# Copying gated products by DMA into 32-bit rounded tiles and transposing them in that type

## The chip, the cores and the metric

The kernel runs on one core of a Trainium2 chip. The core's engines each follow their own instruction stream: TensorE (PE, with PEld for its loads of the stationary operand), VectorE (DVE), ScalarE (ACT), GpSimd (POOL) and SyncE (SP). Data moves between HBM, the on-chip memory SBUF and the accumulation banks PSUM; DMA transfers are issued by one of the engines and carried by 16 DMA engines. The metric is device time in microseconds (us), the median of several runs of the whole program.

## The reference

Two layers of an encoder block on 256 tokens of width 1024. Each layer is a feed-forward half step, two attention branches with gates, and a second feed-forward half step:

```python
for l in range(DEPTH):                                  # DEPTH = 2
    x = x + 0.5 * swiglu(rms_norm(x, ffn1_norm[l]), ffn1_w_gate[l], ffn1_w_up[l], ffn1_w_down[l])
    ...                                                 # neighbourhood and sliding-window attention, gates, w_out
    x = x + 0.5 * swiglu(rms_norm(x, ffn2_norm[l]), ffn2_w_gate[l], ffn2_w_up[l], ffn2_w_down[l])

def swiglu(x, w_gate, w_up, w_down):                    # widths 1024 -> 2816 -> 1024
    return (jax.nn.silu(x @ w_gate) * (x @ w_up)) @ w_down
```

The change touches the four `swiglu` calls: it concerns the product `silu(...) * (...)`, called the gated product here, on its way from the first two matmuls to the third.

## The kernel before, in words

**Numbers in two parts.** Every operand of a matmul is split into a high part rounded to the 32-bit type fp32r and a low part, the rest, also fp32r. `split_to` does it: ACT writes `hi` by a copy (L184), DVE writes `lo = src - hi` (L185). A product then takes three matmuls, hi·hi, hi·lo and lo·hi (`three`, L170 to L172); one such triple of 512 columns is one unit of the kernel's own clock, a tick.

**Feed-forward.** The 2816 middle columns are cut into 11 chunks of 256. For chunk c, `columns` brings the weights in four pieces of 512 KB, gate and up side by side, and `project` forms a 128x512 bank for each of the two token tiles t = 0 and 1: 8 triples a tile, 16 ticks a chunk. `glu` then makes the gated product: ACT applies Silu to one half of the bank (`sg`, L443), DVE multiplies it with the other (`hh`, L444). `hh` has two buffers, each with both token tiles of one chunk.

**The turn.** The third matmul needs the gated product with the middle columns on the partitions. `turn` lets PE transpose two chunks at once (the last chunk, c = 10, alone), as four 128x128 blocks a chunk, against an identity matrix `ident` in float32 (L320), into a PSUM bank `tp`. `arrange` then splits the bank into `hi` and `lo`; for eight of the chunks it first copies it into `a` (L330) and forms four sums for a seven-product scheme of block multiplication. The third matmul follows in `down`, which starts with chunk 0 (eight triples into `acc`).

**What sets the order.** PE's order is the order in which the code records its matmuls. A step that must wait for other engines is put off with `defer(lag, ...)`: it is recorded at the first tick that lies at least `lag` ticks after its call.

```python
H_LAG, NORM_LAG, QK_LAG, P_LAG, V_LAG, M_LAG = 7.9, 4.0, 16, 10, 7.5, 5.5
LAST_LAG = 6.1
...
waiting.append((c, pair[0]))
if c % 2 or c == NFC - 1:
    defer(LAST_LAG if c == NFC - 1 else H_LAG, ("h", c), lambda group=waiting: turn(group))
```

So a pair's turn stands 8 ticks, the last one 7 ticks, behind the last triple of its chunk. On the other engines a scheduler places the instructions. All weight loads are issued by SP into a ring of four raw buffers; a load waits until its buffer has been split, and the splits write a ring of six `wh`/`wl` tiles that PE gives free.

**The opening.** While the first rows of x are on their way, PE runs matmuls on a tile of zeros (`warmup`, L118 to L120): five, then the transposes of the first rows, five more, then the transposes of the rows of token tile 1, then three.

The names that the prediction uses: `hh` the gated product, `tp` the transposes' bank, `wh`, `wl` the parts of a weight piece, `corner`, `u`, `v` pieces of the down weights and their differences for the seven products, `raw` a buffer that a load fills. "FFN 0" to "FFN 3" are the four feed-forward steps in order of time.

Of the kernel before, what the change touches and what calls it, by code (L numbers as in the profile page):

```python
# [11 lines left out]
F32 = mybir.dt.float32  # L12
F32R = mybir.dt.float32r
I32 = mybir.dt.int32
BF16 = mybir.dt.bfloat16
# [6 lines left out]
P = 128  # L22
D = 1024
S = 256
# [5 lines left out]
NFC = FF // FC  # L30
# [10 lines left out]
RING = 6  # L41
RAW = 4
LAG = 3
H_LAG, NORM_LAG, QK_LAG, P_LAG, V_LAG, M_LAG = 7.9, 4.0, 16, 10, 7.5, 5.5
LAST_LAG = 6.1
MORE = {"Q1": 2, ("sw", 4): 1.5, ("na", 4): 2, ("na", 5): 1.5}
ORDER = ("Q0 Q1 K0 K1 q1 q0 a5 k0 a5 k1 a3 v0 a1 a5 v1 a3 g0 a1 a5 g1 a4 g2 a0 g3 a0 a4 g4 a1 a5 g5 a4 "
         "g6 a0 g7")
# [3 lines left out]
PLAN = "SFGFGGFGGSS"  # L52
PREP = {3: 1, 5: 3, 7: 6}
PREP_FIRST = {5: 1, 7: 3, 8: 6}
NS = sum(kind != "S" for kind in PLAN)
# [3 lines left out]
def hybrid_encoder(ctx, tc, x, w_gu1, w_d1, w_in, b_gate, qk_gain, rpb, sink, t5,  # L59
                   w_bna, w_bsw, w_out, w_gu2, w_d2, c_mask, c_band, out):  # L60
    nc = tc.nc
# [7 lines left out]
    ps_tp = ctx.enter_context(tc.tile_pool(name="ps_tp", bufs=2, space=PSUM))  # L69
# [9 lines left out]
    def fetch(t, h):  # L79
        if (t, h) == (0, 0):  # L80
            nc.sync.dma_start(wide[:, :HEAD + 512], x[:P, :HEAD + 512])
        else:
            nc.sync.dma_start(xs[t][:, h * 512:(h + 1) * 512],
                              x[t * P:(t + 1) * P, HEAD + h * 512:HEAD + (h + 1) * 512])
# [3 lines left out]
    ident = const.tile([P, P], F32, name="ident")  # L88
    make_identity(nc, ident)
    ident_r = const.tile([P, P], F32R, name="ident_r")  # L90
# [23 lines left out]
    blank = ring.tile([P, 2, 512], F32R, name="blank", tag="wl", bufs=RING)  # L114
    nc.vector.memset(blank[:, 0, :].bitcast(F32), 0.0)
    idle = ps_acc.tile([P, 512], F32, name="idle", tag="po")

    def warmup(n):  # L118
        for _ in range(n):
            nc.tensor.matmul(idle, blank[:, 0, :P], blank[:, 0, :], start=True, stop=True)  # L120

    chain = {}

# [15 lines left out]
    def load(src, nk, n):  # L139
        raw = ring.tile([P, 2, 512], F32, name="raw", tag="raw", bufs=RAW)  # L140
        r = raw[:, :nk, :n]
        nc.sync.dma_start(r, src)
        return parts(r, nk, n)

    def columns(w, l, c0, n, nk=KD):
        return [load(w[l, 2 * i * P:(2 * i + 2) * P, c0:c0 + n].rearrange("(k p) n -> p k n", p=P), 2, n)
                for i in range(nk // 2)]
# [7 lines left out]
    def defer(lag, key, fn):  # L155
        later.append((now[0] + lag, len(later), key, fn))
        later.sort(key=lambda e: e[0])
# [6 lines left out]
    def tick(cost):  # L164
        now[0] += cost
        while later and later[0][0] <= now[0]:
            later.pop(0)[3]()
# [15 lines left out]
    def split_to(hi, lo, src):  # L183
        linked("act", lambda: nc.scalar.activation(hi, src, AF.Copy))  # L184
        linked("dve", lambda: nc.vector.tensor_tensor(lo, src, hi.bitcast(F32), ALU.subtract))  # L185
# [7 lines left out]
    def norm(t, n, half, apart=False):  # L193
        if half == 0:
            xT[t] = [act.tile([P, KD, P], F32R, name=f"x{p}{t}", tag=f"x{p}{t}") for p in "hl"]
            ssq[t] = small.tile([P, 2], F32, name="ssq", tag="ssq")
        ks = slice(4 * half, 4 * half + 4)
        tp = ps_tp.tile([P, 4, P], F32, name="tp", tag="tp")
        for i in range(4):
            k = 4 * half + i  # L200
            nc.tensor.transpose(tp[:, i, :], xs[t][:, k * P:(k + 1) * P], ident)  # L201
        xg = act.tile([P, 4, P], F32, name="xg", tag="xg", bufs=2)
        if apart and half == 1:
            for i in range(4):
                linked("act", lambda: nc.scalar.activation(xg[:, i, :], tp[:, i, :], AF.Copy,
                                                           scale=gain[:, n, 4 + i:5 + i]))
        else:
            linked("dve", lambda: nc.vector.tensor_tensor(
                xg, tp, gain[:, n, ks].unsqueeze(2).to_broadcast([P, 4, P]), ALU.mult))
        split_to(*(x[:, ks, :] for x in xT[t]), xg)  # L210
        if not apart:
            square(t, half)
# [12 lines left out]
    def opening(w, l, early):  # L225
        def piece(i, c=0):
            return load(w[l, 2 * i * P:(2 * i + 2) * P, c * 512:(c + 1) * 512].rearrange("(k p) n -> p k n", p=P),
                        2, 512)

        ps = [ps_g.tile([P, 512], F32, name="g", tag="g") for _ in range(T)]  # L230

        def steps(t, i):
            wh, wl = pieces[i]
            xh, xl = xT[t]
            for a, b in ((xh, wh), (xl, wh), (xh, wl)):
                for k in (2 * i, 2 * i + 1):
                    nc.tensor.matmul(ps[t], a[:, k, :], b[:, k % 2, :], start=a is xh and b is wh and k == 0,
                                     stop=b is wl and k == KD - 1)
            tick(2)

        pieces = []
        chain["act"] = warmed
        warmup(5)
        norm(0, 0, 0, True)
        pieces.append(piece(0))
        warmup(5)
        fetch(1, 0)
        norm(1, 0, 0, True)
        pieces.append(piece(1))
        fetch(0, 1)  # L250
        fetch(1, 1)
        warmup(3)
        steps(0, 0)
        norm(0, 0, 1, True)
        steps(1, 0)
        pieces.append(piece(2))
        norm(1, 0, 1, True)
        pieces.append(piece(3))
        square(0, 0, idle)
        square(0, 1, idle)  # L260
        for i in (1, 2, 3):
            for t in range(T):
                steps(t, i)
        second = [piece(0, 1)]
        square(1, 0, idle)
        early(ps[0])
        second.append(piece(1, 1))
        square(1, 1, idle)
        second += [piece(i, 1) for i in range(2, KD // 2)]
        chain.clear()  # L270
        defer(24, "constants", constants)
        defer(70, "scaled", scaled)
        return ps, second
# [36 lines left out]
    def ffn(l, n, w_gu, w_d, after):  # L310
        with tc.tile_pool(name="ffn", bufs=1) as fp:
            hs = {}
            SLOT = ((1, 2), (0, 3))

            def turn(group):
                tps = [ps_tp.tile([P, 4, P], F32, name="tp", tag="tp") for _ in group]
                for (_, hh), tp in zip(group, tps):
                    for t in range(T):
                        for i in range(2):
                            nc.tensor.transpose(tp[:, SLOT[t][i], :], hh[:, t, i * P:(i + 1) * P], ident)  # L320
                for (c, _), tp in zip(group, tps):
                    arrange(c, tp)

            def arrange(c, tp):
                m = 4 if PLAN[c] == "S" else 7
                hi = fp.tile([P, m, P], F32R, name=f"hi{m}", tag=f"hi{m}", bufs=NS if m == 7 else NFC - NS)
                lo = fp.tile([P, m, P], F32R, name=f"lo{m}", tag=f"lo{m}", bufs=NS if m == 7 else NFC - NS)
                if m == 7:
                    a = fp.tile([P, 8, P], F32, name="a", tag="sums", bufs=2)
                    nc.scalar.activation(a[:, :4, :], tp, AF.Copy)  # L330
                    for to, x, y, op in ((4, 0, 3, ALU.add), (6, 1, 0, ALU.subtract), (5, 4, 1, ALU.subtract),
                                         (7, 2, 5, ALU.subtract)):
                        nc.vector.tensor_tensor(a[:, to, :], a[:, x, :], a[:, y, :], op)
                    split_to(hi, lo, a[:, 1:, :])
                else:
                    with tc.high_priority(150 if c == NFC - 1 else 0):
                        split_to(hi, lo, tp)
                hs[c] = (hi, lo)
# [108 lines left out]
            waiting = []  # L447
            for c in range(NFC):
                first = n == 0 and c == 0
                pair = [None]  # L450
                if first:
                    both, second = opening(w_gu, l, lambda ps: glu(0, ps, pair))
                elif n == 0 and c == 1:
                    pieces = second
                else:
                    pieces = columns(w_gu, l, c * 512, 512)
                prep = PREP if n else PREP_FIRST
                if c in prep:
                    prepare(prep[c])
                for t in range(T):  # L460
                    if not first:
                        glu(t, project(t, pieces, 512), pair)
                    elif t:
                        glu(t, both[t], pair)
                waiting.append((c, pair[0]))
                if c % 2 or c == NFC - 1:
                    defer(LAST_LAG if c == NFC - 1 else H_LAG, ("h", c), lambda group=waiting: turn(group))
                    waiting = []
# [376 lines left out]
```

## Time and profile before

| what | value |
|---|---|
| median of 3 runs | 1077.5 us (1076.47 to 1078.26) |
| profiled execution: span from first to last instruction | 1075.2 us; no time beside the span is given for this one execution |
| granted TensorE clock, mean | 0.999 |
| PE busy | 1068.2 us, 99% of the span, 5125 matmuls |
| PEld / DVE / ACT / POOL busy | 83% / 81% / 62% / 11% |
| DMA | 212.63 MB moved, mean 198 GB/s; all weight loads on one queue, which took 62.3% of the 16 engines' span |
| chain that ended last | PE 97%, DMA 1%, ACT 1% |

The profile shows one execution. A row of the timeline has start, duration, engine, source line, operation, `out<-in` and the count; what stands in brackets is the engine's idle time just before it and what ended that. Matmuls are pipelined: each lasts longer than the distance to the next, so the distance between starts is what one costs, and a busy PE is not PE at its peak.

### The profile page before, as it was taken

How to read it: one execution, taken by the hardware profiler on the slowest of the kernel's cores; microseconds unless marked ns; L12 is line 12 of the kernel's file. 1: busy time of each engine (PE TensorE's matmuls, PEld its weight loads, DVE VectorE, ACT ScalarE, POOL GpSimd, SP SyncE). 2: the span in 40 equal slices, each digit the busy share in tenths (PEclk: the TensorE clock that was granted, in tenths of full speed). 3: DMA queues.
4: the chain of work that ended last, by engine and by line, in shares of the span. 5: the costliest groups of instructions: out<-in, count | busy, mean ns of one | idle time of the engine just before them, and what ended most of it. 6: DMA issues, size and time to landing. Idle time of an engine off the chain costs nothing.

```text
span 1075.2 us, 14749 instructions
## 1 busy us (share of the span) xinstructions
PE 1068.2 (99%) x5125; PEld 890.3 (83%) x5125; DVE 875.8 (81%) x1337; ACT 671.5 (62%) x1014; POOL 116.7 (11%) x118
## 2 busy tenths in 40 slices
PE   8999999999999999999999999999999999999998
PEld 6888888888888888888888888888888888888887
DVE  6678799889886768869977887988898867778696
ACT  6566654788764556565565665557877646566552
POOL 1000120243520000000000000003534000000000
PEclk9999999999999999999999999999999999999999
DMA  7767656765654667756657765657666554776652
GB/s 247 227 214 237 215 190 191 228 194 155 192 188 137 198 199 246 242 168 191 214 162 238 227 213 185 199 153 247 177 195 185 176 175 160 237 231 203 188 196 89
DMA packets 98827, 212.63 MB, mean 198 GB/s; under 512 B 7568, under 2 KB 13744, under 8 KB 98752
## 3 DMA queue, kind: packets, MB, share of 16 engines
q1 hardware_dynamic: 98560, 211.60, 62.3%
q8 instruction: 40, 0.66, 0.2%
q14 instruction: 35, 0.29, 0.1%
q0 software_dynamic: 192, 0.08, 0.1%
HBM read 210.59 MB, written 1.06 MB: 197 GB/s over the span
## 4 chain that ended last, share of the span: by engine, by line
PE 97%; DMA 1%; ACT 1%; DVE 0%; issue 0%; SPq 0%; ACTq 0%
PE g L170 22%; PE g L172 22%; PE g L171 22%; PE acc L170 5%; PE acc L172 5%; PE acc L171 5%; PE tp L320 2%; PE sc L568 1%; PE po L603 1%; PE tp L170 1%; PE tp L171 1%; PE tp L172 1%; PE pt L589 1%; PE tp L201 1%; PE br L170 1%; PE br L171 1%
## 5 line engine op out<-in xcount | busy, mean ns | idle before, releaser
L185 DVE TENSOR_TENSOR wl<-raw,wh 128x1024 fp32r<-128x1024 f32 x336 | 405.7, 1219 | 65.5 <-ACT wh L184 61.8
L184 ACT ACTIVATE wh<-raw 128x1024 fp32r<-128x1024 f32 x336 | 346.7, 1045 | 117.3 <-DMA raw<-in_w_gu 51.4
L170 PE MATMUL g<-wh,xh 128*128 128x512 f32 (+1 forms) x976 | 383.1, 393 | 0.5 <-DVE hh L444 0.5
L172 PE MATMUL g<-wh,xl 128*128 128x512 f32 (+1 forms) x976 | 377.8, 387 | 0.0
L171 PE MATMUL g<-wl,xh 128*128 128x512 f32 (+1 forms) x976 | 377.5, 387 | 0.0
L172 PEld LDWEIGHTS g<-wh,xl 128*128 128x128 f32 x976 | 183.4, 188 | 39.1 <-DVE xl L185 1.5
L170 PEld LDWEIGHTS g<-wh,xh 128*128 128x128 f32 x976 | 183.6, 188 | 33.8 <-DVE hh L444 1.1
L171 PEld LDWEIGHTS g<-wl,xh 128*128 128x128 f32 x976 | 183.7, 188 | 33.4 <-DVE wl L185 0.6
L443 ACT ACTIVATE sg<-g,rs_y 128x256 f32<-128x256 f32 x88 | 41.1, 467 | 89.7 <-PE g L172 77.3
L444 DVE SCALAR_TENSOR_TENSOR hh<-g,rs_y,sg 128x256 f32<-128x256 f32 x88 | 42.3, 481 | 53.0 <-ACT sg L443 53.0
L170 PE MATMUL acc<-wh,hi 128*128 128x512 f32 x180 | 71.2, 395 | 0.0
L171 PE MATMUL acc<-wl,hi 128*128 128x512 f32 x180 | 70.2, 390 | 0.0
L172 PE MATMUL acc<-wh,lo 128*128 128x512 f32 x180 | 70.1, 390 | 0.0
L176 POOL TENSOR_TENSOR rs_y<-ms,mhalf 128x1 f32<-128x1 f32 x12 | 8.1, 678 | 556.5 <-DVE ms L222 548.0
L352 DVE TENSOR_TENSOR u<-raw 128x512 f32<-128x512 f32 x64 | 41.7, 686 | 20.9 <-DMA raw<-in_w_d 20.8
L184 ACT ACTIVATE corner<-raw 128x512 fp32r<-128x512 f32 x32 | 20.1, 629 | 40.4 <-DMA raw<-in_w_d 22.4
L581 POOL TENSOR_TENSOR S<-S,sm 128x512 f32<-128x512 f32 x32 | 37.2, 1161 | 65.6 <-DVE sm L580 38.3
L172 PEld LDWEIGHTS acc<-wh,lo 128*128 128x128 f32 x180 | 33.8, 188 | 7.2
L171 PEld LDWEIGHTS acc<-wl,hi 128*128 128x128 f32 x180 | 33.8, 188 | 6.7
L170 PEld LDWEIGHTS acc<-wh,hi 128*128 128x128 f32 x180 | 33.8, 188 | 6.7
L184 ACT ACTIVATE wh<-v 128x1024 fp32r<-128x1024 f32 x20 | 21.2, 1062 | 28.9 <-DVE v L352 24.5
L574 ACT ACTIVATE S<-S,mx 128x256 f32<-128x256 f32 x64 | 31.9, 499 | 8.0 <-DVE mx L571 7.9
(189 smaller groups left out, 1522.0 us busy)
## 6 DMA issues: line engine op xcount, KB each, us to landing
raw<-in_w_gu SPq DMA_DIRECT2D x176, 512.0 KB, 4.5
raw<-in_w_d SPq DMA_DIRECT2D x100, 512.0 KB, 4.2
raw<-in_w_in SPq DMA_DIRECT2D x64, 512.0 KB, 4.7
raw<-in_w_out SPq DMA_DIRECT2D x16, 512.0 KB, 3.6
bb<-in_b_gate SPq DMA_DIRECT2D x16, 256.0 KB, 3.6
raw<-in_w_bsw SPq DMA_DIRECT2D x8, 512.0 KB, 3.9
raw<-in_w_bna SPq DMA_DIRECT2D x8, 512.0 KB, 3.5
raw<-in_w_d SPq DMA_DIRECT2D x12, 256.0 KB, 2.7
```

Source lines behind the costliest of these rows:

```text
L170: nc.tensor.matmul(ps, xh, wh, start=first, stop=False)
L171: nc.tensor.matmul(ps, xh, wl, start=False, stop=False)
L172: nc.tensor.matmul(ps, xl, wh, start=False, stop=last)
L184: linked("act", lambda: nc.scalar.activation(hi, src, AF.Copy))
L185: linked("dve", lambda: nc.vector.tensor_tensor(lo, src, hi.bitcast(F32), ALU.subtract))
L201: nc.tensor.transpose(tp[:, i, :], xs[t][:, k * P:(k + 1) * P], ident)
L320: nc.tensor.transpose(tp[:, SLOT[t][i], :], hh[:, t, i * P:(i + 1) * P], ident)
L352: sub = lambda to, x, y: nc.vector.tensor_tensor(to, x, y, ALU.subtract)
L443: linked("act", lambda: nc.scalar.activation(sg, ps[:, :FC], AF.Silu, scale=rstd[t]))
L444: linked("dve", lambda: nc.vector.scalar_tensor_tensor(pair[0][:, t], ps[:, FC:], rstd[t], sg, op0=ALU.mult, op1=ALU.mult))
L574: nc.scalar.activation(S_[:, t, :], S_[:, t, :], AF.Exp, bias=mx[:, t:t + 1], scale=-1.0, accum_out=sm[:, t:t + 1])
L581: nc.gpsimd.tensor_tensor(S_, S_, sm.unsqueeze(2).to_broadcast([P, T, S]), ALU.mult)
```

## The change

1. As soon as the gated product of a chunk is complete, a DMA that ACT issues copies its bits, 128 partitions of 2 KB, into the first four blocks of that chunk's `hi` tile, whose type is fp32r (`bits`). There are 44 such copies, one for each of 11 chunks in four FFNs.
2. PE transposes from there, with the identity in fp32r (`ident_r`) and a bank of type fp32r. The bank is read as float32 afterwards; `hi` is then overwritten with the rounded high part as before.
3. `H_LAG` goes from 7.9 to 10 and `LAST_LAG` from 6.1 to 7.6, so that a pair's turn stands 10 ticks and the last one 8 ticks behind its chunk.
4. The second five warm-up matmuls become two in fp32r, four in bf16 and one in float32, all of 512 columns on the same zeros.

```diff
-H_LAG, NORM_LAG, QK_LAG, P_LAG, V_LAG, M_LAG = 7.9, 4.0, 16, 10, 7.5, 5.5
-LAST_LAG = 6.1
+H_LAG, NORM_LAG, QK_LAG, P_LAG, V_LAG, M_LAG = 10, 4.0, 16, 10, 7.5, 5.5
+LAST_LAG = 7.6
...
-    def warmup(n):
+    def warmup(n, kind=F32R):
+        zero = blank[:, 0, :].bitcast(kind)
         for _ in range(n):
-            nc.tensor.matmul(idle, blank[:, 0, :P], blank[:, 0, :], start=True, stop=True)
+            nc.tensor.matmul(idle, zero[:, :P], zero[:, :512], start=True, stop=True)
...
-        warmup(5)
+        warmup(2)
+        warmup(4, BF16)
+        warmup(1, F32)
         fetch(1, 0)
...
             def turn(group):
-                tps = [ps_tp.tile([P, 4, P], F32, name="tp", tag="tp") for _ in group]
-                for (_, hh), tp in zip(group, tps):
+                tps = [ps_tp.tile([P, 4, P], F32R, name="tp", tag="tp") for _ in group]
+                for (c, raw), tp in zip(group, tps):
                     for t in range(T):
                         for i in range(2):
-                            nc.tensor.transpose(tp[:, SLOT[t][i], :], hh[:, t, i * P:(i + 1) * P], ident)
-                for (c, _), tp in zip(group, tps):
-                    arrange(c, tp)
+                            nc.tensor.transpose(tp[:, SLOT[t][i], :], raw[:, 2 * t + i, :], ident_r)
+                for (c, raw), tp in zip(group, tps):
+                    arrange(c, raw, tp.bitcast(F32))
+
+            def halves(c, p):
+                m = 4 if PLAN[c] == "S" else 7
+                return fp.tile([P, m, P], F32R, name=f"{p}{m}", tag=f"{p}{m}", bufs=NS if m == 7 else NFC - NS)
+
+            def bits(c, hh):
+                hi = halves(c, "hi")
+                nc.scalar.dma_start(hi[:, :4, :].bitcast(F32), hh.rearrange("p t (i n) -> p (t i) n", i=2))
+                return hi
...
-                waiting.append((c, pair[0]))
+                waiting.append((c, bits(c, pair[0])))
```

On PE, the turn of chunks 0 and 1 in FFN 0; before, it stands behind the last triple of chunk 2's tile 0 (`g_371`):

```order
L170 MATMUL g_371<-wh_367,xh0_114 128x512
L171 MATMUL g_371<-wl_368,xh0_114 128x512
L172 MATMUL g_371<-wh_367,xl0_115 128x512
L320 MATMUL tp_396<-ident_83,hh_259 128x128 x4
L320 MATMUL tp_397<-ident_83,hh_315 128x128 x4
L170 MATMUL g_427<-wh_349,xh1_138 128x512
```

and now:

```order
L171 MATMUL g_409<-wh_355,xh1_140 128x512
L172 MATMUL g_409<-wl_356,xh1_140 128x512
L173 MATMUL g_409<-wh_355,xl1_141 128x512
L323 MATMUL tp_416<-ident_r_88,hi4_292 128x128 x4
L323 MATMUL tp_417<-ident_r_88,hi7_351 128x128 x4
L171 MATMUL g_409<-wh_361,xh1_140 128x512
```

It has moved two triples into tile 1 (`g_409`), and it reads `hi` tiles where it read `hh`.

On DVE, the instructions around the last gated product of FFN 0 (chunk 10, tile 1); before:

```order
L352 TENSOR_TENSOR u_1393<-raw_1384,raw_1382 128x512
L185 TENSOR_TENSOR corner_1350<-raw_1346,corner_1350 128x512
L352 TENSOR_TENSOR u_1393<-raw_1382 128x512
L444 SCALAR_TENSOR_TENSOR hh_1242<-g_1193,rs_y_214,sg_1243 128x256
L185 TENSOR_TENSOR corner_1386<-raw_1382,corner_1386 128x512
L333 TENSOR_TENSOR a_1230<-a_1230 128x128 x2
L185 TENSOR_TENSOR lo4_1239<-tp_1219,hi4_1238 128x512
L185 TENSOR_TENSOR wl_1354<-raw_1348,wh_1353 128x1024
L333 TENSOR_TENSOR a_1230<-a_1230 128x128
L185 TENSOR_TENSOR wl_1390<-raw_1384,wh_1389 128x1024
L333 TENSOR_TENSOR a_1230<-a_1230 128x128
L185 TENSOR_TENSOR wl_1397<-u_1393,wh_1396 128x1024
```

(`corner_1432` and then `hh_1242` of tile 1 follow), and now:

```order
L186 TENSOR_TENSOR corner_1363<-raw_1359,corner_1363 128x512
L454 SCALAR_TENSOR_TENSOR hh_1232<-g_1207,rs_y_216,sg_1233 128x256
L186 TENSOR_TENSOR corner_1399<-raw_1395,corner_1399 128x512
L362 TENSOR_TENSOR u_1406<-raw_1397,raw_1395 128x512
L362 TENSOR_TENSOR u_1406<-raw_1395 128x512
L186 TENSOR_TENSOR wl_1367<-raw_1361,wh_1366 128x1024
L343 TENSOR_TENSOR a_1254<-a_1254 128x128 x2
L186 TENSOR_TENSOR lo4_1262<-tp_1244,hi4_1181 128x512
L186 TENSOR_TENSOR wl_1403<-raw_1397,wh_1402 128x1024
L343 TENSOR_TENSOR a_1254<-a_1254 128x128
L186 TENSOR_TENSOR wl_1410<-u_1406,wh_1409 128x1024
L186 TENSOR_TENSOR corner_1445<-raw_1441,corner_1445 128x512
```

(`hh_1232` of tile 1 follows). Two `corner` pieces and tile 0's gated product have moved ahead of `u`, and one of the `a` sums has moved behind the last gated product.

On ACT, the same place; now:

```order
L185 ACTIVATE wh_1409<-u_1406 128x1024
L185 ACTIVATE corner_1445<-raw_1441 128x512
L453 ACTIVATE sg_1283<-g_1236,rs_y_275 128x256
L185 ACTIVATE corner_1477<-raw_1473 128x512
L333 DMA hi4_1286<-hh_1232 128x512
L185 ACTIVATE hi7_1098<-a_1254 128x896
L185 ACTIVATE hi4_1286<-tp_1351 128x512
```

The copy's issue stands behind one more piece of weights (`corner_1477`), and what stood behind that piece now stands behind the copy's issue.

More of the change, by code (lines that the diff above doesn't have):

```diff
@@ L315, in turn, with arrange @@
             def turn(group):
-                tps = [ps_tp.tile([P, 4, P], F32, name="tp", tag="tp") for _ in group]
-                for (_, hh), tp in zip(group, tps):
+                tps = [ps_tp.tile([P, 4, P], F32R, name="tp", tag="tp") for _ in group]
+                for (c, raw), tp in zip(group, tps):
                     for t in range(T):
                         for i in range(2):
-                            nc.tensor.transpose(tp[:, SLOT[t][i], :], hh[:, t, i * P:(i + 1) * P], ident)
-                for (c, _), tp in zip(group, tps):
-                    arrange(c, tp)
-            def arrange(c, tp):
+                            nc.tensor.transpose(tp[:, SLOT[t][i], :], raw[:, 2 * t + i, :], ident_r)
+                for (c, raw), tp in zip(group, tps):
+                    arrange(c, raw, tp.bitcast(F32))
+            def halves(c, p):
                 m = 4 if PLAN[c] == "S" else 7
-                hi = fp.tile([P, m, P], F32R, name=f"hi{m}", tag=f"hi{m}", bufs=NS if m == 7 else NFC - NS)
-                lo = fp.tile([P, m, P], F32R, name=f"lo{m}", tag=f"lo{m}", bufs=NS if m == 7 else NFC - NS)
-                if m == 7:
+                return fp.tile([P, m, P], F32R, name=f"{p}{m}", tag=f"{p}{m}", bufs=NS if m == 7 else NFC - NS)
[3 more added lines that the diff above has]
+                return hi
+            def arrange(c, hi, tp):
+                lo = halves(c, "lo")
+                if PLAN[c] != "S":
                     a = fp.tile([P, 8, P], F32, name="a", tag="sums", bufs=2)
```

## The prediction

> **What bounds the kernel now.** I read the page's busy times and its chain of waits first.
>
> ```profile
> PE 1068.2 (99%) x5125; PEld 890.3 (83%) x5125; DVE 875.8 (81%) x1337; ACT 671.5 (62%) x1014; POOL 116.7 (11%) x118
> PE 97%; DMA 1%; ACT 1%; DVE 0%; issue 0%; SPq 0%; ACTq 0%
> ```
>
> The chain is PE from the opening to the last store. So what PE's own stream loses is gained in full, a wait put into that stream is lost in full, and work on DVE, ACT or the queues counts only where PE comes to wait for it. The last place before PE waits is the splitting of weights, in the groups by line:
>
> ```profile
> L184 ACT ACTIVATE wh<-raw 128x1024 fp32r<-128x1024 f32 x328 | 342.1, 1055 | 116.7 <-DMA raw<-in_w_gu 51.4 <-PE g L172 37.4 <-PE acc L172 11.6
> ```
>
> ACT waits 51 us for loads and about as long for PE to free a tile; none of it reaches PE, because six split pieces lie in between.
>
> **Part 1: the transposes in the rounded type.** How much PE time is one? In the timeline a group of eight stands between triples, here the present ones (37.82 to 39.16) and a group that already uses fp32r, of the queries (227.14 to 228.31):
>
> ```profile
> 37.82 0.39 PE L172 MATMUL g<-wh,xl 128*128 128x512 f32 x1
> 38.05 1.03 PE L320 MATMUL tp<-ident,hh 128*128 128x128 f32 x8
> 38.84 0.48 PE L170 MATMUL g<-wh,xh 128*128 128x512 f32 x1
> 39.16 0.39 PE L171 MATMUL g<-wl,xh 128*128 128x512 f32 x1
> ```
>
> ```profile
> 227.14 0.39 PE L172 MATMUL g<-wh,xl 128*128 128x512 f32 x1
> 227.37 0.80 PE L512 MATMUL tp<-ident_r,qs 128*128 128x128 f32 x8
> 228.01 0.46 PE L170 MATMUL g<-wh,xh 128*128 128x512 f32 x1
> 228.31 0.40 PE L171 MATMUL g<-wl,xh 128*128 128x512 f32 x1
> ```
>
> From the matmul before the group to the second one behind it: 1.34 us in float32, 1.17 us in fp32r, with the same neighbours and the same tile sizes. A group of eight loses 0.17 us. There are 176 transposes, in each FFN five groups of eight and one of four: 20 x 0.17 + 4 x 0.085 = **3.7 us off**. The groups by line give an upper bound:
>
> ```profile
> L320 PE MATMUL tp<-ident,hh 128*128 128x128 f32 x176 | 23.1, 272 | 0.0
> L512 PE MATMUL tp<-ident_r,qs 128*128 128x128 f32 x64 | 6.4, 244 | 0.0
> ```
>
> 23.1 / 176 = 0.131 against 6.4 / 64 = 0.100, or 0.031 x 176 = 5.5 us; but busy time includes the tail that overlaps the next matmul, so I take the distances.
>
> **Part 2: the copies, and when they land.** No copy from SBUF to SBUF and no DMA issued by ACT is in the trace. The nearest rows are the answers on DMA issues (last number: median us from issue to landing) and one issue on SP:
>
> ```profile
> out<-x SPq DMA_DIRECT2D x4, 256.0 KB, 2.0
> raw<-in_w_d SPq DMA_DIRECT2D x12, 256.0 KB, 2.7
> bb<-in_b_gate SPq DMA_DIRECT2D x16, 256.0 KB, 3.6
> 138.84 0.33 SPq L348 DMA_DIRECT2D raw<-in_w_d  x1
> ```
>
> All three move 256 KB, as a copy does. The stores read SBUF, in 128 runs of 2 KB, with nothing beside them: 2.0 us, the lower end. The bias loads, with weight loads in flight, took 3.6: the upper end. A copy reads SBUF like the store and mostly has one load beside it; I take 2.4. The Trainium skill, "DMA: Bandwidth & Descriptors", section "Anatomy of one DMA", fits 2.0 us + bytes / 436e3, that is 2.6 us for 256 KB, on the GpSimd issue path; the store's 2.0 us is below it, and by 2.6 the waits below would come to 1.8 us.
>
> Ordinary turns. The window from the end of the last gated product to the turn is tightest here:
>
> ```profile
> 408.73 0.48 DVE L444 SCALAR_TENSOR_TENSOR hh<-g,rs_y,sg 128x256 f32<-128x256 f32 x1
> 410.73 1.03 PE L320 MATMUL tp<-ident,hh 128*128 128x128 f32 x8
> ```
>
> 410.73 - 409.21 = 1.5 us. The turn now stands two ticks later: 6 matmuls, 6 x 0.227 = 1.36 us (distances above), and the late chunk's four transposes come second, 0.3 us more: 3.2 us for a copy of 2.4. In the new order one weight split (1.06 us) can stand between the last Silu and the copy's issue, so this turn has little left, and the others more. Cost 0 for most; for the few tight ones together 0.3 us (0 to 2). Behind the waiting issue on ACT mostly stands the next chunk's Silu, which waits for PE anyway, so the queue loses little.
>
> The last turns are the tight ones. In FFN 0, DVE and PE:
>
> ```profile
> 130.44 0.69 DVE L352 TENSOR_TENSOR u<-raw 128x512 f32<-128x512 f32 x1 [4.27 <-DMA raw<-in_w_d]
> 131.05 0.69 DVE L185 TENSOR_TENSOR corner<-raw,corner 128x512 fp32r<-128x512 f32 x1
> 132.26 0.48 DVE L444 SCALAR_TENSOR_TENSOR hh<-g,rs_y,sg 128x256 f32<-128x256 f32 x1
> 132.65 0.68 DVE L185 TENSOR_TENSOR corner<-raw,corner 128x512 fp32r<-128x512 f32 x1
> 136.79 0.28 DVE L333 TENSOR_TENSOR a<-a 128x128 f32<-128x128 f32 x1
> 137.00 1.21 DVE L185 TENSOR_TENSOR wl<-u,wh 128x1024 fp32r<-128x1024 f32 x1
> 138.74 0.47 DVE L444 SCALAR_TENSOR_TENSOR hh<-g,rs_y,sg 128x256 f32<-128x256 f32 x1
> 139.77 0.60 PE L320 MATMUL tp<-ident,hh 128*128 128x128 f32 x4
> ```
>
> The product is ready at 139.21 and read at 139.77: 0.56 us. It is late because DVE works without a pause from 130.44 on, after 4.27 us idle. In the new order a `corner` and tile 0's `hh` stand ahead of `u`, where DVE was idle, and one `a` behind the product. That takes off the stretch 131.05 to 132.65 less one `u` (0.61): 0.99, and 0.21 for the `a`: 1.2 us. The turn moves one tick later (0.68) and, by part 1, the turn before it makes it 0.16 earlier. Windows: 0.56 + 1.20 + 0.68 - 0.16 = 2.3 us here; in FFN 1 to 3, from
>
> ```profile
> 489.13 0.48 DVE L444 SCALAR_TENSOR_TENSOR hh<-g,rs_y,sg 128x256 f32<-128x256 f32 x1
> 489.79 0.60 PE L320 MATMUL tp<-ident,hh 128*128 128x128 f32 x4
> 670.02 0.48 DVE L444 SCALAR_TENSOR_TENSOR hh<-g,rs_y,sg 128x256 f32<-128x256 f32 x1
> 671.17 0.60 PE L320 MATMUL tp<-ident,hh 128*128 128x128 f32 x4
> 1020.39 0.48 DVE L444 SCALAR_TENSOR_TENSOR hh<-g,rs_y,sg 128x256 f32<-128x256 f32 x1
> 1021.19 0.60 PE L320 MATMUL tp<-ident,hh 128*128 128x128 f32 x4
> ```
>
> with 0.18, 0.67 and 0.32 us: 1.9, 2.4 and 2.0 us. With copies of 2.0 us PE waits 0.1 us in all, with 2.4 **1.0 us** (0.1 + 0.5 + 0 + 0.4), with 3.6 5.8 us. One more thing stands ahead of this issue: a `corner` that needs a load.
>
> ```profile
> 139.61 0.63 ACT L184 ACTIVATE corner<-raw 128x512 fp32r<-128x512 f32 x1 [1.49 <-DMA raw<-in_w_d]
> ```
>
> That load waits for the buffer that the first `wl` frees, and this `wl` now has `corner`, `hh`, two `a` and `lo` fewer ahead of it, some 2 us; the load should land near 137.5, before the product. If it lands at 139.6 as now, each last turn waits some 1.6 us more.
>
> Traffic. 44 x 0.26 MB = 11.5 MB, 5% more, beside loads; the fullest stretch I found is
>
> ```profile
> 99.00:110.00 11.00, 11.00 (x54) 9.22 (x53) 10.34 (x13) 7.14 (x10) 0.00 (x0) 1.00 0.89 302
> ```
>
> 0.89 of the DMA engines. A delay of half a us a load is hidden by the six split pieces (each lasts PE two ticks, 1.36 us); without that cover it would be up to 0.5 us a chunk. I take 0. `hh` buffers come free at the copy instead of the turn; no engine waits for them now, so nothing is gained.
>
> **Part 3: the opening.**
>
> ```profile
> 4.61 1.65 PE L120 MATMUL idle<-blank 128*128 128x512 f32 x5
> 7.53 0.66 PE L201 MATMUL tp<-ident,x 128*128 128x128 f32 x4 [1.28 <-DMA x<-in_x]
> ```
>
> Five took 1.65 us, then PE waited 1.28 us for x. Seven with one slot each end near 6.9; if float32 takes four slots, near 7.9, 0.4 past the arrival (no row has such a matmul). I take 0 (0 to 0.4).
>
> **The sum.** -3.7 + 1.0 + 0.3 + 0 = -2.4 us: span 1075.2 to 1072.8. The median of the runs lies 2.3 us above that span, so **1075.1 us**. With the ends of the copies it is 1073.9 to about 1080.
>
> **The rivals.**
>
> A. *Late copies at the last turns take it all back (slower).* One mechanism: the issue sits in ACT's in-order queue behind a load, and the copy shares the DMA engines with the weights. It decides from 3.1 us a copy, where the four waits reach 3.7. At 3.6 us: -3.7 + 5.8 + 0.3 = +2.4, 1079.9 us. For: the load at 139.61, and 0.18 us of slack in FFN 1. Against: the store's 2.0 us.
>
> B. *Half of it is lost.* Copies of 2.7 to 3.0 us give waits of 2.2 to 3.4, a net -1.2 to 0: about 1076.9 us, no change that can be told. For: 2.7 is what loads of this size take.
>
> C. *The transposes don't get faster,* because each needs its own load of the stationary operand and eight loads set the pace.
>
> ```profile
> 37.83 1.02 PEld L320 LDWEIGHTS tp<-ident,hh 128*128 128x128 f32 x8
> 227.15 0.88 PEld L512 LDWEIGHTS tp<-ident_r,qs 128*128 128x128 f32 x8
> ```
>
> Then 0 + 1.0 + 0.3: 1078.8 us. Against: eight loads in fp32r take 0.88, not 1.02. The Trainium skill, "TensorE: Matmul & The Clock Gate", section "LDWEIGHTS (loading the stationary operand)", gives columns / 1.2 ns, 107 ns for 128 whatever the type. By that rule eight could not pass in less than 0.85 us; the float32 group's 0.79 us from 38.05 to 38.84 and the fp32r group's 0.64 from 227.37 to 228.01 both do.
>
> **How the numbers follow.** This measurement can tell about 0.2% (2.2 us) from no change. The forecast's case has 0.56; its own range, copies of 2.0 to 2.6 us, is -3.6 to -1.6, and about eight tenths of it, weighed towards the short copies, lies beyond 2.2: 0.46 faster, 0.10 same. B 0.20, nearly all same. A 0.16, nearly all slower. C 0.08, half and half. Together with a small rest: faster 0.48, same 0.34, slower 0.18. The range 1073.3 to 1079.3 reaches from no waits at all to most of A.
>
> **What would show it.** Part 1: eight transposes in fp32r with 1.17 us around them, and PE's stream shorter by 3.7. Part 2: distances above 0.5 us ahead of the last turns, the copies' time to landing, and `hh` of chunk 10 ending some 2.3 us ahead of the turn. Part 3: transposes of x at 7.5 us. Wrong if PE waits at ordinary turns or for `wl`, or if a group of eight still takes 1.34.

## The result, and the profile after the change

The changed kernel takes 1118.8 us (median; 1117.1 to 1120.2) against 1077.6 us (1076.5 to 1078.3) for the kernel before on the same chip: a ratio of 1.038, interval 1.037 to 1.040, or 41 us slower. Forecast was 1075.1 us, with a range up to 1079.3. The profiled execution took 1117.1 us with a span of 1115.3 us, 40.1 us more than the span before. The page of the changed kernel: busy time, the chain of waits, the transposes' group, and the DMA issues.

```profile
PE 1078.7 (97%) x5128; PEld 893.3 (80%) x5128; DVE 879.5 (79%) x1337; ACT 673.8 (60%) x1014; POOL 115.6 (10%) x118
...
PE 65%; DMA 19%; DVE 10%; ACT 3%; issue 3%; POOL 0%; DVEq 0%; ACTq 0%
...
L323 PE MATMUL tp<-ident_r,hi 128*128 128x128 f32 x176 | 21.3, 247 | 31.1 <-DMA hi<-hh 31.1
...
raw<-in_w_gu SPq DMA_DIRECT2D x176, 512.0 KB, 4.5
hi<-hh ACTq DMA_DIRECT2D x44, 256.0 KB, 5.1
```

PE was 97% of the chain; now it is 65%, and DMA 19%. The idle time has one address: PE's transposes wait 31.1 us, all of it for the copies, which take 5.1 us from issue to landing. The answer on tile `hi` gives how often PE waited for a copy (us, times) and the spread of the landings:

```profile
  PE tp L323: 31.1, 20
DMA to landing us min/median/max: 2.2/5.1/7.0
```

Twenty of the 24 turns wait. Measured by the distances between the starts of PE's matmuls (a busy row's modelled end overlaps the next start), the waits are 34.3 us: 26.0 at sixteen ordinary turns, in the middle of the group where the later chunk's copy comes in, and 8.3 at the four last turns. All distances into, within and out of the turns' transposes went from 22.8 to 54.7 us, +31.9. Another +8.1 us lies between matmuls that wait for nothing and run at half speed (last section). The two make 40.0 of the 40.1 us.

**Why a copy takes 5 us.** One late copy, chunk 3 of FFN 1, in the timeline (start, duration, instruction):

```profile
421.90 2.35 DVE L186 TENSOR_TENSOR wl<-raw,wh 128x1024 fp32r<-128x1024 f32 x2
424.17 0.48 DVE L454 SCALAR_TENSOR_TENSOR hh<-g,rs_y,sg 128x256 f32<-128x256 f32 x1
...
424.28 1.94 SPq L358 DMA_DIRECT2D raw<-in_w_d  x2
...
424.68 0.47 ACTq L333 DMA_DIRECT2D hi<-hh  x1
...
428.39 0.46 PE L323 MATMUL tp<-ident_r,hi 128*128 128x128 f32 x4
431.21 0.53 PE L323 MATMUL tp<-ident_r,hi 128*128 128x128 f32 x4 [2.36 <-DMA hi<-hh]
```

The product ends at 424.65 and the copy is issued 0.03 us later, so ACT's queue is not at fault (the issue comes as promptly at 37 of the 44 copies). But `hh` stands on DVE right behind a `wl`. The end of that split frees a `raw` buffer, SP answers with a load of 512 KB at 424.28, and the copy follows 0.4 us behind it: so it is at 21 of the 24 late copies, 0.7 to 1.1 us at the other three. Two answers on DMA, the first from 436 to 442 us, the second from 423 to 433 us (KB each, us to landing):

```profile
raw<-in_w_gu SPq DMA_DIRECT2D x2, 512.0 KB, 3.6
hi<-hh ACTq DMA_DIRECT2D x1, 256.0 KB, 2.2
...
raw<-in_w_d SPq DMA_DIRECT2D x2, 512.0 KB, 5.9
hi<-hh ACTq DMA_DIRECT2D x1, 256.0 KB, 6.5
```

The copy at 438.65 comes when the loads are nearly through: its first packet (the first piece of its data that moves) starts 1.14 us after the issue, and it has landed at 2.2. The one at 424.68 starts at 2.7 us and lands at 6.5. In the median over all 44 the first packet starts 2.6 us after the issue.

That a load goes ahead is not the whole cause. At 414.59 and 964.58 us a copy was issued with no load less than 2.4 us ahead of it; its first packet started at 1.1 us, but a load followed 0.5 and 0.6 us behind it, and it landed after 4.6 and 4.4 us. (A third such copy, at 605.19, landed after 2.5.) So a copy with no load just ahead of it isn't short for that alone.

### The profile page after: what moved, and what is told of

It reads as the page before. It is cut to its first block, busy times and chain, and to the rows that moved or that the text cites. A ratio compares the mean times of both kernels' runs of the same rounds, so it can differ in the third digit from the quotient of the medians.

```text
span 1115.3 us, 14873 instructions
## 1 busy us (share of the span) xinstructions
PE 1078.7 (97%) x5128; PEld 893.3 (80%) x5128; DVE 879.5 (79%) x1337; ACT 673.8 (60%) x1014; POOL 115.6 (10%) x118
## 4 chain that ended last, share of the span: by engine, by line
PE 65%; DMA 19%; DVE 10%; ACT 3%; issue 3%; POOL 0%; DVEq 0%; ACTq 0%
PE g L171 12%; PE g L173 12%; PE g L172 12%; DMA hi<-hh 8%; DMA raw<-in_w_gu 6%; DVE wl L186 5%; PE acc L173 5%; PE acc L172 5%; PE acc L171 5%; DMA raw<-in_w_d 4%; ACT wh L185 3%; DVE u L362 1%; PE sc L578 1%; PE po L613 1%; PE tp L172 1%
## 5 line engine op out<-in xcount | busy, mean ns | idle before, releaser
L171 PEld LDWEIGHTS g<-wh,xh 128*128 128x128 f32 x976 | 185.1, 190 | 34.3 <-DVE hh L454 0.6
L323 PE MATMUL tp<-ident_r,hi 128*128 128x128 f32 x176 | 21.3, 247 | 31.1 <-DMA hi<-hh 31.1
L323 PEld LDWEIGHTS tp<-ident_r,hi 128*128 128x128 f32 x176 | 18.4, 140 | 37.6 <-DMA hi<-hh 25.7
```

Source lines behind the costliest of these rows:

```text
L171: nc.tensor.matmul(ps, xh, wh, start=first, stop=False)
L323: nc.tensor.transpose(tp[:, SLOT[t][i], :], raw[:, 2 * t + i, :], ident_r)
```

## The experiments

Times are medians beside runs of the kernel before in the same comparison.

**Is it the loads in flight, or the copy itself? (e5, e6)** e5 cuts the copy; e6 cuts the loads.

```diff
-                nc.scalar.dma_start(hi[:, :4, :].bitcast(F32), hh.rearrange("p t (i n) -> p (t i) n", i=2))
+                nc.scalar.dma_start(hi[:, 2 * t:2 * t + 2, :].bitcast(F32), hh[:, t].rearrange("p (i n) -> p i n", i=2))
```

> The change with each copy cut in two, one half for each token tile, issued as soon as that tile's product is ready; what is left to land late is 128 KB instead of 256 KB. Theory (a late copy's time is set by the weight loads that are in flight when it is issued, one of them issued 0.4 us ahead of it; its own bytes take some 0.9 us of it): a late half still takes 4.2 to 4.8 us from issue to landing, the waits of 34 us become 22 to 29 us: 1104 to 1113 us. Rival (a copy from SBUF to SBUF is slow by itself, in proportion to its bytes): half of 5.1 us, waits below 3 us: 1076 to 1079 us.

Measured 1099.1 us (ratio 1.020, 1.019 to 1.022). The row of the copies on the page:

```profile
hi<-hh ACTq DMA_DIRECT2D x88, 128.0 KB, 4.2
```

Halved bytes take 4.2 us instead of 5.1; the second halves, which come late, take 4.5. So most of the time does not go with the bytes. The waits are 22.8 us, as expected; the time lies below the expected range because only one slow stretch is left of five.

```diff
-        nc.sync.dma_start(r, src)
-        return parts(r, nk, n)
+        nc.sync.dma_start(r[:, :1, :], src[:, :1, :])
+        return parts(r[:, :1, :].to_broadcast([P, nk, n]), nk, n)
```

(and the same for the rows of `in_w_d`)

> The change with every weight load after the first ones cut to its first half (256 KB instead of 512 KB; the splits read that half twice, so the second half of the weights is left out), the copies as they are. Theory (the copies queue behind the loads): first packet 1.2 to 2.0 us after the issue instead of 2.6, landing 2.5 to 3.6 us instead of 5.1, PE waits below 8 us: 1076 to 1086 us. Rival (the copies are slow by themselves, or ACT's queue is): landing 4.5 to 5.5 us, waits about 34 us, about 1115 us.

Measured 1077.2 us in one run. The DMA issues on its page:

```profile
raw<-in_w_gu SPq DMA_DIRECT2D x176, 256.0 KB, 2.7
hi<-hh ACTq DMA_DIRECT2D x44, 256.0 KB, 3.2
```

and who waited for tile `hi` (us, times):

```profile
  PE tp L323: 3.2, 4
```

With the loads halved the same copies land at 3.2 us, between 2.7 and 3.8, and all waits at ordinary turns are gone; the last four turns wait 3.2 us. The copy's time is set by the loads around it, and that settles the cause of the waits. How much of it is due to a load ahead and how much to one behind was not tried.

**Does it cost time when PE doesn't wait for it? (e2)**

```diff
+                hi = halves(c, "hi")
+                nc.scalar.dma_start(hi[:, :4, :].bitcast(F32), pair[0].rearrange("p t (i n) -> p (t i) n", i=2))
-                waiting.append((c, pair[0]))
+                waiting.append((c, pair[0], hi))
```

> The kernel before with its lags, its opening and its float32 transposes of the products themselves; the 44 copies are issued as in the change into the tile of the high parts, and no transpose reads them (the split that fills that tile later still waits for them). Theory (only PE's wait for a copy costs time; the traffic and the issues on ACT are hidden): 1077 to 1079 us, PE waits below 1 us in all, copies landing about 5 us after issue as in the change. Rival (the copies delay the weights, and the weights delay PE): over 1083 us, with PE waits ahead of projections.

Measured 1079.9 us (1.0021, 1.0012 to 1.0030): 2.3 us, not 41. The answer on tile `hi`, idle time of an engine before it, and the spread:

```profile
  DMA hi<-hh: 14.6, 4
DMA to landing us min/median/max: 3.3/5.3/6.6
```

The copies are as slow as in the change, so the turn doesn't cause that. The small loss can't be put down to traffic alone: at the four last turns ACT's split waits 14.6 us for the copy, which stands ahead of the weights' splits there. PE itself waits 1.0 us for `hi` behind the last turn of FFN 3 and 2.0 us for `x` at the ends of the FFNs (by distances); the kernel before has neither wait.

**Does each turn wait until a landing that is fixed? (e3, e4)** Only the lags change: e3 has `H_LAG` 12, e4 15 and `LAST_LAG` 10.6.

```diff
-H_LAG, NORM_LAG, QK_LAG, P_LAG, V_LAG, M_LAG = 10, 4.0, 16, 10, 7.5, 5.5
-LAST_LAG = 7.6
+H_LAG, NORM_LAG, QK_LAG, P_LAG, V_LAG, M_LAG = 15, 4.0, 16, 10, 7.5, 5.5
+LAST_LAG = 10.6
```

> The change with its ordinary turns two ticks later (12 instead of 10), the last turns where they are. Theory (each turn waits from its place until the late chunk's copy lands, and the landing does not depend on the turn's place): each ordinary wait 1.36 us shorter or gone, 26.0 us of them become 7.5; with the last turns' 8.3 us 15.8 us are left, of the slow stretches 0 to 3; about 1096 us (1093 to 1099). Rival (the landing moves with the turn, since the turn's own work holds up the copy): waits as long as before, about 1118 us.

> The change with its ordinary turns five ticks later (15 instead of 10) and its last turns three ticks later (10.6 instead of 7.6). Theory: 3.4 us more for a copy at ordinary turns and 2.0 us more at the last ones; waits of 0.5 us in FFN 0 and 0.1 us elsewhere are left, no slow stretch: 1074 to 1076 us. Rival (the loads that collide with the copies leave PE short of weights, or the late turn holds up the next chunk): over 1079 us with waits at other lines.

e3: 1105.4 us (1.026, 1.025 to 1.027); e4: 1079.9 us (1.0029, 1.0017 to 1.0040). PE's waits for `hi` in e3 and in e4:

```profile
  PE tp L323: 19.5, 13
```

```profile
  PE tp L323: 5.0, 4
```

The ordinary waits shrink nearly as expected, from 26.0 us to 9.8 (expected 7.5) and 0.7 (by distances, as above). Both miss at the last turns: there the waits rose to 11.4 us in e3 instead of staying at 8.3, and are 5.2 in e4 instead of 0.6. A later ordinary turn puts its `a` and `lo` nearer to the last product on DVE and ACT, and in FFN 0 and 3 that product is later too. In FFN 0 it ended 3.8 us behind the start of its chunk's last matmul in the change, 5.0 in e3 and 5.2 in e4; there it was ready at 139.68, for a turn due at 142.18. In FFN 1 and 2 it came at most 0.2 us later than in the change, and e4's waits there are short (0.2 and 0.6 us). e4's time is its rival's, but most of PE's waiting is still at the turns. Slow stretches: 6.0 us in e3, 1.4 in e4.

**Is the slow stretch behind a wait due to idle time? (e7)** At the ordinary turns, ahead of the second chunk's transposes:

```diff
+                    if n:
+                        fill = ps_acc.tile([P, 512], F32, name="fill", tag="po")
+                        for _ in range(12):
+                            nc.tensor.matmul(fill, ident_r, xT[0][0][:, :4, :], start=True, stop=True)
```

> The change with 12 matmuls of 512 columns (2.72 us, their result read by nobody) between the two chunks' transposes at the 20 ordinary turns, where PE otherwise waits. Theory (the slow stretches of 0.427 us a matmul follow where PE idled): 54.5 us of matmuls added, the ordinary waits of 26 us gone but for 0.5 us, no slow stretch behind an ordinary turn: about 1141 us (1139 to 1144). Rival (the stretches come with the copies or the transposes, not with idle time): four stretches stay behind ordinary turns, 6 us more, 1146 us or more.

Measured 1148.4 us in one run: above the theory's range, where the rival had it. But the rival's sign, slow stretches behind ordinary turns, is not there. Who waited for tile `hi`:

```profile
  PE tp L327: 12.5, 4
```

PE waits at the four last turns alone (13.2 us by distances, 4.9 more than assumed, which is most of the miss), and the three slow stretches left all follow these. None follows a filled turn, though the copies are as many and as slow (5.2 us). So neither copies nor transposes bring them on; in this run only idle time did.

**What are the shorter transposes worth? (e1, e12, e13, e14)** e1 has no copies and waits for none:

```diff
-                    pair[0] = act.tile([P, T, FC], F32, name="hh", tag="xg", bufs=2)
+                    pair[0] = act.tile([P, T, FC], F32R, name="hh", tag="xg", bufs=2)
-                            nc.tensor.transpose(tp[:, SLOT[t][i], :], hh[:, t, i * P:(i + 1) * P], ident)
+                            nc.tensor.transpose(tp[:, SLOT[t][i], :], hh[:, t, i * P:(i + 1) * P], ident_r)
```

> The kernel before with its lags and its opening; the gated products are written by VectorE into tiles of the rounded type (so their low bits are dropped, which is the part of the computation that is left out) and transposed as that type; no copies. Theory (part 1 of the prediction stands, the copies alone cost time): eight transposes take 1.17 us between their neighbours, PE waits nowhere, about 3.6 us off: 1074.0 us. Rival (the shorter groups bring a new wait, of ACT or DVE behind the turn, which is part of the loss): 1077 us or more, with PE waits around the turns.

Measured 1078.9 us, slower than before (1.0015, 1.0007 to 1.0024). All twenty groups of eight take 1.165 to 1.175 us, so PE's part came as predicted. It is lost at the ends of the FFNs, where PE waits for `x`. Who waited for tile `x`, first in the kernel before (its one wait is in the opening), then in e1:

```profile
  PE tp L201: 1.3, 1
```

```profile
  PE tp L201: 4.6, 6
```

The chain of waits of e1 from 176 to 187 us (start, us, what):

```profile
by line: DMA raw<-in_w_in 45.5%; issue 13.7%; DVE wl L185 11.5%; DVE x L424 10.9%; ACT wh L184 9.7%; DVE x L304 6.2%; DVE ends L419 5.4%; DVEq L419 0.4%; ACTq L184 0.2%
...
177.53 5.00 DMA raw<-in_w_in
...
182.62 1.07 ACT wh L184
...
183.71 0.04 DVE wl L185
...
184.85 0.68 DVE x L304
```

A load of 5.0 us, its two splits, and only then the update of `x` for which PE waits. Is it the order on DVE, or the load? e12 puts that split behind the update (e11 below does the same for another kernel):

```diff
+            with tc.issue_after(after.ins) if after is not None and i else ExitStack():
+                out.append(load(w[l, 2 * i * P:(2 * i + 2) * P, c0:c0 + n].rearrange("(k p) n -> p k n", p=P), 2, n))
```

> The run e1 (rounded products, float32r transposes, no copies; the products' low bits are left out) with the same change of order on VectorE as in e11. Theory: of e1's waits ahead of x's transposes (5.5 us above the ordinary distances) less than 2 us are left, 1074 to 1076 us, so that part 1's gain shows. Rival (the loads are late whatever the order): 1078 us or more.

Measured 1079.2 us (1.0021, 1.0012 to 1.0030); PE still waits for `x`, 4.9 us. The order on DVE only decides where: ahead of the first transposes of `x` at the ends of FFN 0 to 2 PE waits 1.3 us instead of 4.4 (by distances), ahead of the later ones 4.4 instead of 1.1. Changing the order moves the wait and doesn't end it. e13 and e14 cut the loads as in e6, in the kernel before and in e1.

> The kernel before with every weight load cut to its first half (256 KB, read twice by the splits; the second half of the weights is left out). Theory (PE bounds the kernel before, no load does): 1076 to 1078 us as with whole loads. Rival (the loads hold the kernel before somewhere): 1075 us or less.

> The run e1 (products rounded when written, float32r transposes, no copies) with every weight load cut in the same way; against e13. Theory (at the ends of the FFNs the weights come just in time, so that a PE that arrives earlier waits for the loads behind x's update; with short loads part 1's gain shows in full): 3.0 to 3.8 us below e13, waits ahead of x's transposes below 1 us. Rival (the gain is lost to VectorE's and ACT's order alone): as far above e13 as e1 is above the kernel before, or at most 1 us below it, with the waits of 5 us ahead of x's transposes still there.

e13 takes 1076.1 us, e14 1072.8 us: **3.4 us** between them, and in e14 no wait of PE for `x` is left. So part 1's gain exists, and at the full length of the loads the ends of the FFNs take it back. Why e1 loses even more than it gains is only partly seen: in FFN 0 the loads of the down projection are issued up to 2.2 us later than before (166.44 for 164.26 us, and the last one 172.86 for 171.38) although PE is ahead; what starts that delay was not tried.

**Can it be mended? (e8 to e11)** e8 leaves the last chunk of each FFN as before and gives the others more time:

```diff
-                tps = [ps_tp.tile([P, 4, P], F32R, name="tp", tag="tp") for _ in group]
+                tps = [ps_tp.tile([P, 4, P], F32 if c == NFC - 1 else F32R, name="tp", tag="tp") for c, _ in group]
-                waiting.append((c, bits(c, pair[0])))
+                waiting.append((c, pair[0] if c == NFC - 1 else bits(c, pair[0])))
-                    defer(LAST_LAG if c == NFC - 1 else H_LAG, ("h", c), lambda group=waiting: turn(group))
+                    defer(LAST_LAG if c == NFC - 1 else 10 if c == NFC - 2 else 14, ("h", c), lambda group=waiting: turn(group))
```

> The change with the last chunk of each FFN as before (no copy, float32 transposes of the product itself), the turn of chunks 8 and 9 at lag 10 as in the change, and the other ordinary turns at lag 14. Theory: copies of up to 6.2 us land in time at the turns at lag 14; waits of 0.5 to 1.5 us in all, 20 groups of eight 0.17 us shorter each: 1074 to 1076 us. Rival (the later turns move the work of DVE and ACT so that something else comes late, as in the two runs with turns moved or shortened): 1078 us or more.

> The run with the last chunk as before (e8), with the ordinary turns at lag 15, the turn of chunks 8 and 9 at lag 12 and the last turn one tick later (8.6). Theory (what kept e8 at the time before is 3.5 us of waits and a slow stretch behind one of them, 1.9 us of it at the one turn left at lag 10): waits below 0.8 us, no slow stretch, 1074 to 1075.5 us. Rival (the later turns move DVE's and ACT's work so that weights come late for PE elsewhere): 1076.5 us or more, with waits ahead of x's transposes or of projections.

> The run with the last chunk as before (e8), with each copy in two halves as in e5, ordinary turns at lag 14, the turn of chunks 8 and 9 at lag 12. Theory: late halves land 4.5 us after issue, at most 6.3, the turns leave them some 5.9 us: waits below 0.6 us in all, 1074 to 1075.5 us. Rival (as in e9, or the doubled issues on ACT hold up its queue): 1076.5 us or more.

> The run e9 with one order changed on VectorE: the split of the second weight piece of the stage after an FFN comes behind the first update of x at the FFN's end instead of ahead of it. Theory (what e9 still loses is PE's wait for x, whose update stands on VectorE behind a split that waits for a late load; 2.1 us above the ordinary distances in e9's profile): those waits below 0.8 us, 1074.3 to 1075.6 us. Rival (the loads at the FFN's end are late for PE whatever the order; the wait only moves to the next projections): 1076 us or more, with the same time lost there.

e8: 1076.9 us (1.0000, 0.9991 to 1.0009); e9: 1076.2 (0.9994, 0.9985 to 1.0003); e10: 1076.7 (0.9997, 0.9989 to 1.0006); e11: 1076.4 (0.9991, 0.9982 to 1.0000). In e8 3.1 us of waits for copies were left, 1.9 of them in FFN 0 at the turn of chunks 8 and 9, which is still at lag 10. In e9 PE waits 0.7 us for copies but 2.1 us for `x`, as its rival had it; in e11 1.4 and 1.0, and the time stayed 0.8 us above its range. In e10 it waits 1.3 us for a copy, where less than 0.6 was expected, and 2.1 for `x`. No run reached its theory's time. The 41 us are gone, and a gain that can be told from none is not there: e11's interval ends at 1.0000.

## Why the prediction was wrong

**The failed step is the price of a copy**, "I take 2.4", with 2.0 and 3.6 us as its ends. It measured 5.1 us, from 2.2 to 7.0. The lower end was right for a copy with little beside it (2.2). The upper end came from the bias loads, whose 3.6 is a median over issues with and without company: in the trace of the kernel before, four of the sixteen took 5.0 to 5.5 us, each with a load of `in_w_in` issued within 1.6 us of it. The nearer rows stood on the same page, the weight loads of these stretches:

```profile
raw<-in_w_gu SPq DMA_DIRECT2D x176, 512.0 KB, 4.5
raw<-in_w_d SPq DMA_DIRECT2D x100, 512.0 KB, 4.2
```

A transfer that shares the engines with them takes its time from them (e6). The prediction gave a copy "mostly" one load beside it; at the late copies of the ordinary turns two or three were in flight when the copy was issued, at the last turns one. It asked how many bytes a copy moves and not what is issued around it. Before the change, too, a `wl` stood ahead of `hh` on DVE; that it frees a buffer, and that SP's load is then issued 0.4 us ahead of the copy, could have been followed there.

**The windows were nearly right, and so was the way to the waits.** At the last turns 2.3, 1.9, 2.4 and 2.0 us were given; from the end of the product to the transposes' place it was 1.9, 2.2, 2.2 and 2.4. FFN 1 in the timeline of the changed kernel:

```profile
510.85 0.47 DVE L454 SCALAR_TENSOR_TENSOR hh<-g,rs_y,sg 128x256 f32<-128x256 f32 x1
...
511.35 0.47 ACTq L333 DMA_DIRECT2D hi<-hh  x1
...
513.30 0.39 PE L173 MATMUL acc<-wh,lo 128*128 128x512 f32 x1
515.58 0.51 PE L323 MATMUL tp<-ident_r,hi 128*128 128x128 f32 x4 [1.90 <-DMA hi<-hh]
```

511.32 to 513.53, where the next start would be at 0.227 us, is 2.2; the copy landed 4.1 us after its issue. For ordinary turns "3.2 us" was the tight end; they had 2.8 to 5.6. With 5.1 us a copy the prediction's own sum is 4 x 5.1 - 8.6 = 11.8 us at the last turns (measured 8.3) and up to 5.1 - 3.2 = 1.9 us at each ordinary one (measured 1.6 in the mean of the sixteen that wait). "Cost 0 for most" fell with the price.

**Rival A** named the right kind of wait and the right side, from 3.1 us a copy on, but looked for it at the last turns alone and gave 1079.9. Its first half, the issue held up on ACT behind a load, did not happen: 0.03 us at three of the four last turns, 0.35 at the fourth.

**Part 1** was right for PE: a full group of eight that waits for nothing, in the same timeline,

```profile
503.04 0.39 PE L173 MATMUL g<-wh,xl 128*128 128x512 f32 x1
503.26 0.81 PE L323 MATMUL tp<-ident_r,hi 128*128 128x128 f32 x8
503.90 0.46 PE L171 MATMUL g<-wh,xh 128*128 128x512 f32 x1
504.20 0.39 PE L172 MATMUL g<-wl,xh 128*128 128x512 f32 x1
```

has 1.16 us from 503.04 to 504.20, and e14 against e13 shows 3.4 of the 3.7 us; rival C is out. The Trainium skill, "TensorE: Matmul & The Clock Gate", section "LDWEIGHTS (loading the stationary operand)", gives columns / 1.2 ns for a load, an estimate of 107 ns for 128. The loads of the float32 transposes, started 108 to 110 ns apart, agree with it, so the prediction's 0.79 us was no case against the rule; those of the fp32r ones, 82 to 90 ns apart, do not. Wrong was the prediction's first paragraph, where what PE's stream loses "is gained in full": at the ends of the FFNs the weights come just in time, and e1 shows that a PE that arrives earlier only waits there. A chain that is 97% PE doesn't say how much slack the other chains have.

**Traffic at 0** can't be parted from the rest: e2's 2.3 us hold ACT's waits too. The loads' own medians moved from 4.2 to 4.5 (`in_w_d`) and not at all (`in_w_gu`).

**Part 3** was right at 0. The timeline of the opening:

```profile
4.61 3.05 PE L121 MATMUL idle<-blank 128*128 128x512 f32 x8
7.49 0.60 PE L202 MATMUL tp<-ident,x 128*128 128x128 f32 x4
```

Seven warm-up matmuls stand as eight rows; the last two start 0.43 us apart and end the group, so the float32 one took about four slots. It fitted: x's transposes stand at 7.49 instead of 7.53, the first projection at 8.63 instead of 8.73: 0.1 us gained, alone not told apart by a timing.

## What to carry to other kernels

Price a new transfer by rows of transfers that run in the same stretch, and follow what is issued around it: here the split that stood ahead of the product on DVE freed a buffer, and at 21 of the 24 late copies the load that fills it was issued first. A hand-over from one engine to another that becomes a DMA needs a window as long as the loads in flight take, here 5 to 7 us, where a direct read at the last turns made do with 0.2 to 0.7. And before a gain of the busiest engine is counted, look at the places where another chain arrives just in time.

## What the hardware showed that was not expected

PE's granted clock fell to half in five stretches of 3.41 us behind waits, and stayed full behind other waits that were as long. The later four start 75.06, 112.68, 389.18 and 627.97 us behind the first one, at 43.41, which is 21.99, 33.01, 114.02 and 183.98 times 3.413 us: a fixed grid of windows that doesn't start with the wait. Busy time by such windows, changed kernel (stretch; length; PE busy; the column behind POOL is the granted clock):

```profile
40.00:43.41 3.41, 1.38 (x8) 1.20 (x9) 1.99 (x3) 1.19 (x3) 0.00 (x0) 1.00 0.80 267
43.41:46.82 3.41, 3.41 (x10) 2.64 (x9) 1.60 (x4) 1.06 (x1) 0.00 (x0) 0.51 0.30 115
87.78:91.19 3.41, 2.11 (x12) 1.61 (x11) 2.01 (x3) 2.02 (x3) 0.00 (x0) 1.00 0.98 336
91.19:94.61 3.42, 1.97 (x11) 1.71 (x12) 1.92 (x7) 0.60 (x1) 0.00 (x0) 1.00 0.86 286
94.61:98.02 3.41, 3.41 (x17) 2.82 (x16) 2.79 (x6) 3.34 (x4) 0.00 (x0) 1.00 0.13 50
...
644.11:647.52 3.41, 1.72 (x10) 1.50 (x11) 2.14 (x6) 1.31 (x3) 0.00 (x0) 1.00 0.72 214
647.52:650.94 3.42, 3.42 (x17) 2.81 (x16) 2.80 (x6) 3.10 (x4) 0.00 (x0) 1.00 0.35 127
667.97:671.38 3.41, 1.68 (x13) 1.32 (x12) 1.63 (x3) 2.05 (x3) 0.00 (x0) 1.00 0.76 283
671.38:674.80 3.42, 3.42 (x10) 2.64 (x9) 1.83 (x5) 1.15 (x2) 0.00 (x0) 0.52 0.52 155
```

Of a wait of 2.9 us, 2.0 lay in the window from 40.00; PE was busy for 1.38 us of that window, and the next one ran at 0.51. A wait as long, at 89.73, was halved by a border, with 2.11 and 1.97 us busy on its two sides, and the clock stayed at 1.00. The nearest pair is 1.72 us busy (clock stays) against 1.68 (clock falls): about half a window. So it went at all twenty waits of this execution: the clock fell behind the five with 1.89 us or more of waiting inside one window and behind none of the others, with 1.65 or less. In e7 it did not go so once: a window from 719.69 with 1.57 us busy was followed by one at 1.00. Near half a window, then, busy time alone doesn't decide, and what else does stays open. One such window costs PE some 1.6 us, eight matmuls at 0.427 instead of 0.227 us. The Trainium skill, "TensorE: Matmul & The Clock Gate", section "Part 1: The HAM clock gate (the "warmup" mystery)", states a free-running window of 3413 ns, which this grid shows; it lets the clock fall after an idle window, where in the changed kernel's run a window idle for more than about half was enough.

The Trainium skill, "DMA: Bandwidth & Descriptors", section "Queues, rings and completion order", has each DMA engine take turns between queues at packets. By that, a copy on ACT's queue should start beside the loads of SP's; here its first packet came 2.6 us after the issue in the median. It came at 1.1 us at the four copies ahead of which the last load had been issued 2.4 us or more before, though that load was still moving; at 1.4 to 1.5 where it was 1.5 us before; and at 1.6 to 4.0 where it was 1.1 us or less. What holds it until then was not tried, nor was a copy issued on SP's own queue.
